# A state-space prologue on 64x64 quadrants of the PE array, with its input B laid out anew and ScalarE's early squares moved

## The chip, the cores and the metric

One core of a Trainium2 chip. The time is the device time of one execution in microseconds. Engines: PE (TensorE matmul), DVE (VectorE), ACT (ScalarE), POOL (GpSimd), SP (SyncE, which only issues DMAs; ACT issues some too).

## The reference, cut to what matters

T = 256 positions of 2048 channels pass through a state-space layer (S5), a SwiGLU feed-forward layer, a dilated attention layer and a second feed-forward layer. Only the first is touched:

```python
u = rms_norm(x, g)                       # 128 groups of 16 channels, 64 states a group
dt = exp(log_dt); a = exp(lam * dt)      # complex, worked out as pairs re, im
bb = ((a - 1) / lam)[..., None] * b      # den = lr*lr + li*li stands below the line
s[t] = a * s[t-1] + bb @ u[t]            # per group, an associative scan over t
y = Re(c @ s[t]) + d * u
z = gelu(y); val, gate = split(z @ w_glu)
x = x + val * sigmoid(gate)
```

## The kernel before, in words

The kernel is one program in a fixed order: each engine executes its instructions in the order in which the code writes them, and waits on semaphores in between. Its long part is `stream`, which reads each weight matrix in 128x1024 pieces, splits a piece into hi (ACT, L722 or L726) and lo (DVE), and does six matmuls of 512 columns per piece and half of T (`mm`, L744, L745, L748). The first job of the stream is GLU (`z @ w_glu`), and `later(d, f)` puts a task between its steps. The stream's loads begin during the prologue, at the calls `next(st)`.

Ahead of it is the prologue: `s5_load` (L191) issues the loads, `s5_params` (L238) works out a from lam and dt on DVE, and `s5` (L356) does the layer. The groups go in pairs, 64 pairs q in four sets k of 16; a tile has two halves of 64 partitions, g2, one per group of the pair. T is cut into 64 chunks of four positions, so that the scan runs over 64 chunk states `vs` (64 chunks, re and im, 64 pairs). The pieces:

- start: the parameters `par` (lam, log dt), B (`bt`, with the norm's gain `gb`), C (`ct`), x by rows (`xr`) and by channels (`xu`) are loaded; on ACT stand L371 (a negated copy of `gb`), four row squares L377 for the norm, L393, and then the two squares of lam, L259 (`den`) and L260 (`l2`), inside `s5_params`. On POOL stand memsets of zero blocks, the products L381 and L382 of B with the gain, and L387 (`dm`). DVE runs `exp_steps`: its third operation writes a bank that L259's tile shares.
- `w_build(k, q0, n)` (DVE, L447 to L457): per power j, two products and a sum, the matrices W.
- per unit u of 8 pairs: `v_trans` (PE transposes of W, ACT copies L466 and L467 into `wpad`, a half of the partitions each, zeros beside), `v_build` (PE L476, W times u; ACT copies L480 into `vs`).
- `q_build` (POOL, three operations per power t, `cmul`, L234 to L236): C times powers of a, into a `stage`, from which DMAs (L442) put each half into a tile `qp` with zero blocks.
- `k_build`, `t_build` (PE L493, then DMAs L510): the products inside a chunk, as a table `tz` per pair.
- the scan: `l1` (three levels inside four chunks), `l2` (one after another over 14 steps, small operations of 64 elements, L137), `l3` (three levels outward); `level` writes four operations, L523 to L526. `l1([3])` is POOL's. `coefs` (ACT, L551) copies the coefficients that DVE's scan reads into a bank.
- `t_part(k)` (PE L594) and `s_part(k)` (PE L608, gelu on ACT L610) sum y of a set into two banks; `z_part(k)` transposes z (PE L149), and splits it into hi (ACT L624) and lo (DVE).

Zero blocks make one matmul of 128 rows serve the two groups of a pair, which do not mix: with rows of both groups the columns of the other are zero. A `tile_position` of (0, 64h) puts it into one half of the array's columns.

The order at the end, on PE: t_part(0), t_part(1), s_part(0), z_part(0), s_part(1), t_part(2), t_part(3), s_part(2), s_part(3), GLU, with z_part(1) to z_part(3) as tasks inside GLU. On DVE: w_build, l1 of sets 0 and 1, l2(0) with l1 of 2, l3(0), l2(1) with l3(1), l3(2), l3(3). On POOL: q_build(0) and (1), l1([3]), q_build(2), q_build(3), one level of l3(3).

Of the kernel before, what the change touches and what calls it, by code (L numbers as in the profile page):

```python
# [55 lines left out]
def layouts(i):  # L56
# [5 lines left out]
    col = lambda v: np.broadcast_to(v.reshape(2, 1, 32, 2, 16), (2, 4, 32, 2, 16)).transpose(0, 1, 4, 2, 3).reshape(128, 64)  # L62
# [37 lines left out]
class Trunk:  # L100
# [90 lines left out]
    def s5_load(self):  # L191
# [8 lines left out]
        self.bt = za[:, 0:3072].rearrange("p (c r q) -> p c r q", c=16, r=3)  # L200
# [3 lines left out]
        nc.scalar.dma_start(self.bt[:, :, 0:2, :], a["bt"].rearrange("p (c r q) -> p c r q", c=16, r=2))  # L204
# [17 lines left out]
        pools = {True: [self.scr() for _ in range(2)], False: [self.wtile(w, F32) for w in ("hi", "lo", "lo")]}  # L222
# [14 lines left out]

    def s5_params(self, rms):  # L238
# [5 lines left out]
        homes = [[self.bank(i), 0] for i in (0, 1, 2, 3)]  # L244
        ins = self.small

        def ps(w):
            h = next(h for h in homes if h[1] + w <= 512)
            h[1] += w
            return h[0][:, h[1] - w:h[1]]  # L250

# [3 lines left out]
        zz, mags, k2, ang, l2, dens = [ins(64) for _ in range(6)]  # L255
        den, kk = ps(64), ps(64)
# [99 lines left out]
    def s5(self, st):  # L356
# [6 lines left out]
        wpad = self.p_x.tile([128, 2, 8, 2, 128], F32, tag="x", name="wpad")  # L363
        blank = lambda eng, v: [eng.memset(v[64 * g2:64 * g2 + 64, 2048 - 2048 * g2:4096 - 2048 * g2], 0.0) for g2 in range(2)]
# [28 lines left out]
        nc.scalar.activation(bt[:, :, 2, :], bt[:, :, 0, :], AF.Copy, scale=-1.0)  # L393
# [15 lines left out]
        for g2 in range(2):  # L409
            o = self.qp[64 * g2:64 * g2 + 64, 1, 2048 - 2048 * g2:4096 - 2048 * g2]  # L410
            nc.scalar.copy(o.rearrange("p (a b) -> p a b", b=64), bc(vs[64 * g2:64 * g2 + 64, 0, 0, :], [64, 32, 64], [1]))
# [16 lines left out]
        def q_build(k, ts):  # L428
# [4 lines left out]
            work = ptmp if k < 2 else [zb[:, 3072 + 512 * c:3584 + 512 * c] for c in range(2)]  # L433
            for t in ts:
                so = stage[k // 2][t // 2][:, 512 * (t % 2):512 * (t % 2) + 512]
                self.cmul(pool, v4(so), bc(self.lam[:, t, 1, qs], sh, [1, 1]),
                          bc(self.lam[:, t, 2, qs], sh, [1, 1]), ct[:, :, 1:3, qs], ct[:, :, 0:2, qs], v4(work[0]), v4(work[1]))
                if t % 2:
                    for g2 in range(2):
                        pr = slice(64 * g2, 64 * g2 + 64)  # L440
                        c = 2048 * g2 + 512 * t - 512
                        nc.sync.dma_start(qp[k][pr, c:c + 1024], stage[k // 2][t // 2][pr])  # L442

        stage = [[self.wtile(w, F32) for w in ("hi", "lo")]]
        w4 = lambda v, n: v[:, 0:32 * n].rearrange("p (c r q) -> p c r q", c=16, r=2)

        def w_build(k, q0, n):  # L447

            qs = slice(16 * k + q0, 16 * k + q0 + n)
            sh = [128, 16, 2, n]  # L450
            for j in range(5):
                if j < 4:
                    tt(w4(t1p[j % 2], n), bc(self.g[:, j, 0, qs], sh, [1, 1]), bt[:, :, 0:2, qs], mul)
                    tt(w4(dtmp[j % 2], n), bc(self.g[:, j, 1, qs], sh, [1, 1]), bt[:, :, 1:3, qs], mul)
                if j > 0:
                    tt(wt(k, q0, n)[:, :, :, j - 1, :].rearrange("p q r c -> p c r q"),
                       w4(t1p[(j - 1) % 2], n), w4(dtmp[(j - 1) % 2], n), add)  # L457

        def v_trans(u):
            k, e = u // 2, u % 2  # L460
            for f in range(2):
                ps = self.bank(f)
                for i in range(4):
                    self.tr(ps[:, 128 * i:128 * i + 128], wt(k, 8 * e + 4 * f + i)[:, 0].rearrange("p r j c -> p (r j c)"))
                pv4 = ps.rearrange("p (q m) -> p q m", q=4)
                nc.scalar.copy(wpad[0:64, e, 4 * f:4 * f + 4, 0, :], pv4[0:64])  # L466
                nc.scalar.copy(wpad[64:128, e, 4 * f:4 * f + 4, 1, :], pv4[64:128])  # L467

        def v_build(u):
# [12 lines left out]

        cd = usw.rearrange("p q n -> p (q n)")
        qp = [self.qp[:, 0], self.qp[:, 1], cd, self.qp[:, 0]]

        def k_build(k):

            h, b = k // 2, k % 2
            for i in range(16):
                o = kk[b][64 * h:64 * h + 64, 32 * i:32 * i + 32]  # L490
                for ri in range(2):
                    c0 = 64 * (16 * k + i) + 32 * ri
                    nc.tensor.matmul(o, wt(k, i)[:, 0, ri].rearrange("p j c -> p (j c)"), cd[:, c0:c0 + 32], start=False,  # L493
                                     stop=(i == 15 and ri == 1), tile_position=(0, 64 * h))
            nc.scalar.copy(kt[64 * h:64 * h + 64, :, b].rearrange("p g q c -> p q g c"),
                           kk[b][64 * h:64 * h + 64].rearrange("p (q g c) -> p q g c", q=16, g=2))

        def t_tile(t, n):

            for e in range(n // 16):  # L500
                nc.scalar.copy(t[:, 2048 * e:2048 * e + 2048].rearrange("p (a b) -> p a b", b=64),
                               bc(vs[:, 0, 0, :], [128, 32, 64], [1]))
            return t.rearrange("p (m q c) -> p m q c", m=8, c=16)

        def t_build(t, h, bs):
# [82 lines left out]
        def t_part(k, tz, nq):  # L588
            py = [self.bank(2 - 2 * (k % 2) + e) for e in range(2)]
# [557 lines left out]
```

## Time and profile before

| | before |
|---|---|
| median of 3 runs | 2258.2 us (2256.35 to 2258.35) |
| the profiled execution, its own time | 2256.78 us |
| its span in the trace | 2255.0 us |
| granted TensorE clock, mean | 0.99 of full speed |
| PE busy | 2154.6 us (96%) |
| DVE, ACT, POOL busy | 1546.1, 1035.3, 196.8 us |
| first matmul of GLU | at 170.15 us of the span |

Busy time is an average over the prologue and a stream more than ten times as long; POOL's 196.8 us lie almost all in the prologue. The trace counts two records for one fp32 matmul.

### The profile page before, as it was taken

How to read it: one execution, taken by the hardware profiler on the slowest of the kernel's cores; microseconds unless marked ns; L12 is line 12 of the kernel's file. 1: busy time of each engine (PE TensorE's matmuls, PEld its weight loads, DVE VectorE, ACT ScalarE, POOL GpSimd, SP SyncE). 2: the span in 40 equal slices, each digit the busy share in tenths (PEclk: the TensorE clock that was granted, in tenths of full speed). 3: DMA queues.
4: the chain of work that ended last, by engine and by line, in shares of the span. 5: the costliest groups of instructions: out<-in, count | busy, mean ns of one | idle time of the engine just before them, and what ended most of it. 6: DMA issues, size and time to landing. Idle time of an engine off the chain costs nothing.

```text
span 2255.0 us, 27355 instructions
## 1 busy us (share of the span) xinstructions
PE 2154.6 (96%) x10520; PEld 1791.5 (79%) x10520; DVE 1546.1 (69%) x2648; ACT 1035.3 (46%) x1177; POOL 196.8 (9%) x166
## 2 busy tenths in 40 slices
PE   1769999999999999999999999999999999999998
PEld 1658888888888888878888888877888888888886
DVE  7785777776777675574877687677776776774544
ACT  3714445444444443433545545535444444444443
POOL 6930000000000000000000000000000000000000
PEclk9979999999999999999999999999999999999999
DMA  5425555555555555555554444445555555555553
GB/s 166 109 88 206 190 189 214 187 188 204 187 188 201 191 202 190 186 187 195 191 186 177 143 173 159 150 167 181 193 189 203 189 191 199 188 214 196 201 188 131
DMA packets 60563, 410.37 MB, mean 182 GB/s; under 512 B 7248, under 2 KB 8144, under 8 KB 12816
## 3 DMA queue, kind: packets, MB, share of 16 engines
q1 hardware_dynamic: 58176, 400.13, 49.8%
q10 hardware_dynamic: 1968, 6.92, 0.9%
q8 instruction: 82, 1.34, 0.2%
q0 software_dynamic: 288, 1.57, 0.2%
q14 instruction: 49, 0.40, 0.1%
HBM read 398.90 MB, written 2.10 MB: 178 GB/s over the span
## 4 chain that ended last, share of the span: by engine, by line
PE 88%; DVE 8%; issue 2%; ACT 1%; DMA 1%; SPq 0%; ACTq 0%; DVEq 0%
PE b L745 28%; PE b L744 28%; PE b L748 28%; DVE scr L814 2%; DVE lo L137 1%; PE b L608 1%; DVE b L137 1%; PE b L149 1%; PE b L1037 1%; ACT hi L722 1%; DMA qp<-in_xr 1%; DVE raw L137 1%; PE b L1068 1%; DVE b L523 0%; DVE b L525 0%
## 5 line engine op out<-in xcount | busy, mean ns | idle before, releaser
L146 DVE SCALAR_TENSOR_TENSOR lo<-raw,gcol,hi 128x1024 fp32r<-128x1024 f32 x464 | 594.5, 1291 | 324.2 <-ACT hi L726 318.1
L744 PE MATMUL b<-hi,xt 128*128 128x512 f32 x1856 | 726.2, 391 | 1.7 <-ACT hi L726 1.4
L745 PE MATMUL b<-lo,xt 128*128 128x512 f32 x1856 | 722.7, 389 | 0.9 <-DVE lo L146 0.9
L726 ACT ACTIVATE hi<-raw,gcol 128x1024 fp32r<-128x1024 f32 x464 | 525.1, 1148 | 398.3 <-PE b L748 378.1
L748 PE MATMUL b<-hi,xt 128*128 128x512 f32 x1856 | 571.8, 389 | 0.0
L137 DVE TENSOR_TENSOR lo<-raw,hi 128x1024 fp32r<-128x1024 f32 x272 | 335.7, 1239 | 304.4 <-ACT hi L722 303.0
L722 ACT CAST hi<-raw 128x1024 fp32r<-128x1024 f32 x272 | 283.5, 1052 | 315.3 <-PE b L748 305.9
L744 PEld LDWEIGHTS b<-hi,xt 128*128 128x128 f32 x1856 | 348.5, 188 | 73.8 <-ACT hi L726 1.8
L748 PEld LDWEIGHTS b<-hi,xt 128*128 128x128 f32 x1856 | 348.4, 188 | 73.1
L745 PEld LDWEIGHTS b<-lo,xt 128*128 128x128 f32 x1856 | 348.5, 188 | 72.5 <-DVE lo L146 1.8
L745 PE MATMUL b<-lo,ht 128*128 128x512 f32 x704 | 274.3, 390 | 2.5 <-DVE lo L137 2.5
L744 PE MATMUL b<-hi,ht 128*128 128x512 f32 x704 | 274.0, 389 | 0.1
L814 DVE STREAM_TRANSPOSE scr<-scr 32x128 f32<-32x128 f32 x704 | 212.9, 302 | 11.3
L748 PE MATMUL b<-hi,ht 128*128 128x512 f32 x704 | 217.2, 389 | 0.0
L745 PEld LDWEIGHTS b<-lo,ht 128*128 128x128 f32 x704 | 132.1, 188 | 31.5 <-DVE lo L137 4.0
L744 PEld LDWEIGHTS b<-hi,ht 128*128 128x128 f32 x704 | 132.1, 188 | 27.7 <-ACT hi L722 0.5
L748 PEld LDWEIGHTS b<-hi,ht 128*128 128x128 f32 x704 | 132.1, 188 | 27.5
L818 POOL TENSOR_TENSOR ht<-scr,ht 128x512 fp32r<-128x512 f32 x44 | 57.0, 1296 | 880.9 <-ACT ht L817 852.4
L817 ACT CAST ht<-scr 128x512 fp32r<-128x512 f32 x44 | 27.3, 621 | 178.5 <-DVE scr L814 178.5
L745 PE MATMUL b<-lo,z 128*128 128x512 f32 x256 | 100.1, 391 | 0.5 <-DVE lo L137 0.5
L814 DVE STREAM_TRANSPOSE scr<-x 32x128 f32<-32x128 f32 x320 | 96.8, 302 | 4.9
L744 PE MATMUL b<-hi,z 128*128 128x512 f32 x256 | 100.0, 391 | 0.0
(205 smaller groups left out, 1475.2 us busy)
## 6 DMA issues: line engine op xcount, KB each, us to landing
raw<-in_fi SPq DMA_DIRECT2D x176, 1024.0 KB, 4.8
raw<-in_fo SPq DMA_DIRECT2D x88, 1024.0 KB, 4.8
raw<-in_wq SPq DMA_DIRECT2D x48, 1024.0 KB, 4.8
raw<-in_glu SPq DMA_DIRECT2D x32, 1024.0 KB, 4.8
raw<-in_wo SPq DMA_DIRECT2D x16, 1024.0 KB, 4.8
raw<-in_kv SPq DMA_DIRECT2D x8, 1024.0 KB, 4.8
qp<-in_xr SPq DMA_DIRECT2D x4, 512.0 KB, 10.9
xw<-in_xu SPq DMA_DIRECT2D x4, 512.0 KB, 11.3
```

Of the source, the lines that this page charges most:

```text
L137: self.nc.vector.tensor_tensor(out, in0, in1, op)
L146: self.nc.vector.scalar_tensor_tensor(out, in0, s, in1, op0, op1)
L149: self.nc.tensor.transpose(out, in_, self.ident[:n, :n])
L608: nc.tensor.matmul(py[e][64 * h:64 * h + 64, 128 * i:128 * i + 128], vs[:, :, ri, 16 * k + q], w[:, :, ri, q], start=False, stop=(i == 3 a ...
L722: nc.scalar.copy(hi, raw)
L726: nc.scalar.activation(hi, raw, AF.Copy, scale=gk)
L744: nc.tensor.matmul(ps[b], xh, hi[:, c], start=first, stop=False)
L745: nc.tensor.matmul(ps[b], xh, lo[:, c], start=False, stop=False)
L748: nc.tensor.matmul(ps[b], xl, hi[:, c], start=False, stop=last)
L814: nc.vector.transpose(out[32 * q:32 * q + 32, :, 32 * a:32 * a + 32], src[32 * a:32 * a + 32, :, q, :])
L817: nc.scalar.copy(dst(0), out)
L818: nc.gpsimd.tensor_tensor(dst(1), out, dst(0).bitcast(F32), ALU.subtract)
```

## The change

**Quadrants.** `v_build`, `k_build`, `t_part` and `s_part` use 64 rows and 64 columns of the array for each matmul (`tile_position=(64*row, 64*col)`), one group of a pair in each row half, so there are no zero blocks: `wpad` becomes `wT` (two copies of 128x512 per unit in place of four of 64x512), and `cd` (an input of 2 MB), its four DMAs, the fills of `tz`, `qp` and `cd` by ACT are gone. The columns that a matmul streams halve (128 to 64 in `t_part` and `s_part`; 32 to 16 in `k_build`), and there are twice as many. A bank now belongs to a row half g2, and gelu reads by g2.

**Q in place.** `q_build` writes straight into `qp` (four sets in two tiles of half size) with no stage and no DMA.

**B laid out for W.** `bt` goes from (c, r, q) to (r, q, c): the DMA is 8 KB a row, and `w_build`'s operations run over 16 adjacent elements in c.

**ACT.** `s5_homes` holds the squares of lam ahead of L371's copy and the row squares; `coefs(0)` comes after unit 3.

**Order.** q_build(0), (1), (2), then l1([3]), then q_build(3) on POOL; t_part(2) behind s_part(0), t_part(3) behind s_part(1); z_part(0) and z_part(1) ahead of s_part(2), through bank 5 alone, with a full copy on ACT and lo on POOL; z_part(2) and (3) as tasks of GLU; `next(st)` earlier; two of l3(3)'s levels as 8 operations of 480 elements for 16 of 240.

The diff's core (`k_build`, `t_build` and `v_trans` follow the same pattern):

```diff
 def s5_load
-        nc.scalar.dma_start(self.bt[:, :, 0:2, :], a["bt"].rearrange("p (c r q) -> p c r q", c=16, r=2))
+        nc.scalar.dma_start(za[:, 0:2048], a["bt"])
...
+    def s5_homes(self):
...
+        self.den, self.li2 = ps(64), self.small(64)
+        self.nc.scalar.activation(self.den, self.par[:, 0:64], AF.Square)
+        self.nc.scalar.activation(self.li2, self.par[:, 64:128], AF.Square)
...
 def s5_params
-        nc.scalar.activation(den, lr, AF.Square)
-        nc.scalar.activation(l2, li, AF.Square)
...
 def s5
-        pool.memset(wpad[0:64, :, :, 1, :], 0.0)
-        pool.memset(wpad[64:128, :, :, 0, :], 0.0)
-        blank(pool, self.qp[:, 0])
+        pool.memset(tz, 0.0)
         nc.scalar.activation(self.rq[:, 0:1], vs[:, 0, 0, 0:1], AF.Sqrt)
+        self.s5_homes()
+        nc.scalar.activation(ngb, self.gb, AF.Copy, scale=-1.0)
...
         def w_build(k, q0, n):
-                    tt(w4(t1p[j % 2], n), bc(self.g[:, j, 0, qs], sh, [1, 1]), bt[:, :, 0:2, qs], mul)
+                    tt(w4(t1p[j % 2], n), bc(self.g[:, j, 0, qs], sh, [2, 2]), bq[:, qs, 0:2], mul)
-                    tt(wt(k, q0, n)[:, :, :, j - 1, :].rearrange("p q r c -> p c r q"),
-                       w4(t1p[(j - 1) % 2], n), w4(dtmp[(j - 1) % 2], n), add)
+                    tt(wt(k, q0, n)[:, :, :, j - 1, :], w4(t1p[(j - 1) % 2], n), w4(dtmp[(j - 1) % 2], n), add)
...
         def v_build(u):
+                    for g2 in range(2):
+                        nc.tensor.matmul(pv[ri][half(g2), 64 * i:64 * i + 64], wT[e][half(ri), i, half(g2)],
+                                         (upp if ri == g2 else usw)[half(ri), q0 + i, :], start=True, stop=True,
+                                         tile_position=(64 * ri, 64 * g2))
...
+            if u == 3:
+                coefs(0, 5)
+        coefs(1, 7)
+        for k in range(3):
+            q_build(k)
         go(l1([0, 1], dve))
...
         go(l1([3], pool))
+        q_build(3)
...
         def t_part
-                        nc.tensor.matmul(py[e][64 * h:64 * h + 64, 128 * i:128 * i + 128], upp[:, q, :], tz[:, :, q % nq, :],
-                                         start=(i == 0), stop=False, tile_position=(0, 64 * h))
+                        for g2 in range(2):
+                            nc.tensor.matmul(py[g2][half(h), 64 * (4 * e + i):64 * (4 * e + i) + 64], upp[half(g2), q, :],
+                                             th[k // 2][half(g2), :, 16 * (q % 32):16 * (q % 32) + 16],
+                                             start=(e == 0 and i == 0), stop=False, tile_position=(64 * g2, 64 * h))
...
         def s_part
-                            nc.tensor.matmul(py[e][64 * h:64 * h + 64, 128 * i:128 * i + 128], vs[:, :, ri, 16 * k + q],
-                                             w[:, :, ri, q], start=False, stop=(i == 3 and ri == 1), tile_position=(0, 64 * h))
+                            for g2 in range(2):
+                                nc.tensor.matmul(py[g2][half(h), 64 * (4 * e + i):64 * (4 * e + i) + 64],
+                                                 vs[half(g2), :, ri, 16 * k + q], qv[k][half(g2), :, ri, q], start=False,
+                                                 stop=(e == 1 and i == 3 and ri == 1), tile_position=(64 * g2, 64 * h))
...
         def z_part
+                if copy:
+                    nc.scalar.copy(full, src)
+                    pool.tensor_tensor(low, full, hi.bitcast(F32), sub)
...
         s_part(0, py[0])
-        q_build(3, range(4))
-        lo = z_part(0, (7, 2))
-        l31 = l3(1)
-        go(l2(1), l31)
-        go(lo)
+        py.append(t_part(2, 2))
+        go(l2(1), l3(1))
         s_part(1, py[1])
-        py += [t_part(2, tq[0], 16), t_part(3, tq[1], 16)]
-        next(st)
+        py.append(t_part(3, 0))
         go(l3_level(3, 3, pool))
         go(l3(2))
-        go(pipe([l3_level(3, i, dve, q0, 8) for q0 in (0, 8) for i in range(1, 3)]))
+        for k in range(2):
+            z_part(k, (5, 5), True)
         s_part(2, py[2])
+        go(pipe([l3_level(3, i, dve) for i in range(1, 3)]))
         next(st)
         s_part(3, py[3])
```

The first rows of ACT. Names: `hi_84` holds the parameters, `lo_88` is gb, `z_86` bt, `qp` the rows of x. Before:

```order
L370 ACT_TABLE_LOAD
L370 ACTIVATE rq<-vs 128x1
L371 ACTIVATE z_86<-lo_88 128x1024
L377 ACTIVATE qp,ss<-qp 128x1024 x4
L393 ACTIVATE z_86<-z_86 128x16x64
L259 ACTIVATE b_129<-hi_84 128x64
L260 ACTIVATE hi_108<-hi_84 128x64
```

With the change:

```order
L368 ACT_TABLE_LOAD
L368 ACTIVATE rq<-vs 128x1
L245 ACTIVATE b_114<-hi_84 128x64
L246 ACTIVATE hi_108<-hi_84 128x64
L370 ACTIVATE z_86<-lo_88 128x1024
L376 ACTIVATE qp,ss<-qp 128x1024 x4
L391 ACTIVATE z_86<-z_86 128x1024
```

The two squares of lam (L259, L260; now L245, L246) have moved from behind six operations to the front.

POOL where l1([3]) begins (`vs` is the chunk states, `lo_249` and `lo_243` the working tile, `scr` holds coefficients and powers). Before:

```order
L234 TENSOR_TENSOR lo_249<-scr_106,z_87 128x512
L235 TENSOR_TENSOR lo_249<-scr_106,z_87 128x512
L236 TENSOR_TENSOR lo_253<-lo_249 128x512
L523 TENSOR_TENSOR lo_249<-scr_107,vs 128x512
L524 TENSOR_TENSOR lo_249<-scr_107,vs 128x512
L525 TENSOR_TENSOR lo_249<-lo_249,vs 128x512
L526 TENSOR_TENSOR vs<-lo_249 128x16x2x16
```

With the change:

```order
L230 TENSOR_TENSOR lo_243<-scr_106,z_87 128x512
L231 TENSOR_TENSOR lo_243<-scr_106,z_87 128x512
L232 TENSOR_TENSOR qp<-lo_243 128x512
L508 TENSOR_TENSOR lo_243<-scr_107,vs 128x512
L509 TENSOR_TENSOR lo_243<-scr_107,vs 128x512
L510 TENSOR_TENSOR lo_243<-lo_243,vs 128x512
L511 TENSOR_TENSOR vs<-lo_243 128x16x2x16
```

What is written is now `qp` and not the stage, and 36 such operations of `q_build` stand ahead of l1([3]) where there were 24.

ACT at the end of the prologue (`xw` receives z, `z_1157` and `z_1509` hi of z; L610 and L598 are gelu). Before:

```order
L610 ACTIVATE xw<-b_972 128x8x4x16
L610 ACTIVATE xw<-b_973 128x8x4x16
L624 CAST z_1157<-b_1158 128x512
L624 CAST z_1157<-b_1164 128x512
L610 ACTIVATE xw<-b_990 128x8x4x16
L610 ACTIVATE xw<-b_991 128x8x4x16
L610 ACTIVATE xw<-b_1274 128x8x4x16
L610 ACTIVATE xw<-b_1275 128x8x4x16
L722 CAST hi_1382<-raw_1310 128x1024
```

With the change:

```order
L598 ACTIVATE xw<-b_1111 128x8x4x16
L598 ACTIVATE xw<-b_1112 128x8x4x16
L614 CAST z_1509<-b_1510 128x512
L617 COPY xw<-b_1510 128x512
L614 CAST z_1509<-b_1518 128x512
L617 COPY xw<-b_1518 128x512
L614 CAST z_1509<-b_1526 128x512
L617 COPY xw<-b_1526 128x512
L614 CAST z_1509<-b_1534 128x512
L617 COPY xw<-b_1534 128x512
L598 ACTIVATE xw<-b_1291 128x8x4x16
```

The gelu of set 1 (b_1111, b_1112) is now followed by four pairs of copies, two for each of z_part(0) and z_part(1), ahead of the gelu of set 2 (b_1291); before, two copies of z_part(0) stood ahead of the gelu of set 1 (b_990).

## Rows read from the trace of the kernel before

**Rows 1.** The page, 40 equal slices of the span, two engines.

```profile
PE   1769999999999999999999999999999999999998
...
POOL 6930000000000000000000000000000000000000
```

**Rows 2.** PE in order of time, 140 to 171 us (start, length, line, count, releaser).

```profile
140.82 1.94 PE L149 MATMUL b<-cst,xw 128*128 128x128 f32 x8 [7.92 <-DVE b L137]
144.22 7.71 PE L608 MATMUL b<-qp,vs 128*64 128x128 f32 x64 [1.46 <-DVE vs L526]
151.67 3.76 PE L594 MATMUL b<-raw,xw 128*64 128x128 f32 x64
...
170.15 0.50 PE L744 MATMUL b<-hi,z 128*128 128x512 f32 x1
```

**Rows 3.** Order of time on DVE, 30 to 160 us.

```profile
35.28 0.43 DVE L137 TENSOR_TENSOR b<-b,z 128x256 f32<-128x256 f32 x1
...
71.46 1.12 DVE L137 TENSOR_TENSOR z<-b,dtmp 128x256 f32<-128x256 f32 x2
83.45 0.70 DVE L523 TENSOR_TENSOR b<-b,vs 128x512 f32<-128x512 f32 x1 [10.86 <-ACT b L551]
...
125.08 0.67 DVE L523 TENSOR_TENSOR b<-b,vs 128x480 f32<-128x480 f32 x1
```

**Rows 4.** Order of time on DVE, 0 to 20 us.

```profile
4.44 1.98 DVE L143 TENSOR_SCALAR hi<-hi 128x64 f32<-128x64 f32 x2 [4.44 <-DMA hi<-in_par]
17.11 0.23 DVE L141 TENSOR_SCALAR b<-hi 128x64 f32<-128x64 f32 x1 [10.69 <-ACT b L259]
17.37 1.47 DVE L141 TENSOR_SCALAR hi<-hi 128x64 int32<-128x64 int32 x1
...
18.89 0.18 DVE L141 TENSOR_SCALAR hi<-hi 128x64 int32<-128x64 int32 x1
```

**Rows 5.** Order of time on ACT and its issues (ACTq), 0 to 182 us.

```profile
1.94 4.87 ACTq L205 DMA_DIRECT2D cst<-in_consts  x1
6.85 1.28 ACT L370 ACT_TABLE_LOAD   x1 [6.85 <-issue]
...
16.87 0.21 ACT L259 ACTIVATE b<-hi 128x64 f32<-128x64 f32 x1
...
82.08 0.34 ACTq L648 DMA_DIRECT2D xw<-in_cd  x1
...
141.95 0.59 ACT L624 CAST z<-b 128x512 fp32r<-128x512 f32 x1 [8.41 <-PE b L149]
```

**Rows 6.** Order of time on POOL, 0 to 52 us.

```profile
11.85 2.35 POOL L381 TENSOR_TENSOR z<-z,lo 128x1024 f32<-128x1024 f32 x1 [3.64 <-DMA z<-in_bt]
...
16.86 1.92 POOL L387 TENSOR_TENSOR lo<-cst,hi 128x1024 f32<-128x1024 f32 x1
```

**Rows 7.** Groups by shape, 0 to 175 us (count, busy us, mean ns, idle before).

```profile
L466 ACT COPY wpad<-b 64x512 f32<-64x512 f32 x16 | 9.5, 595 | 5.3 <-PE b L149 5.1
...
L137 DVE TENSOR_TENSOR raw<-b,dtmp 128x512 f32<-128x512 f32 x8 | 8.1, 1046 | 0.0
...
L526 DVE TENSOR_TENSOR vs<-b,dtmp 128x512 f32<-128x512 f32 x6 | 4.1, 678 | 0.0
```

**Rows 8.** Order of time on POOL, 50 to 99 us.

```profile
50.29 1.27 POOL L234 TENSOR_TENSOR lo<-scr,z 128x512 f32<-128x512 f32 x1
...
83.17 1.27 POOL L523 TENSOR_TENSOR lo<-scr,vs 128x512 f32<-128x512 f32 x1 [1.44 <-ACT vs L480]
...
97.08 1.20 POOL L526 TENSOR_TENSOR vs<-lo 128x480 f32<-128x480 f32 x1
```

**Rows 9.** PE at 71 us; L608 by stretch (busy, count, granted clock, DMA share, GB/s).

```profile
71.51 2.09 PE L476 MATMUL b<-xw,wpad 128*64 128x64 f32 x64 [0.40 <-ACT vs L480]
...
125.10:127.00 1.90, 1.90 (x16) 0.50 0.00 0
157.00:160.00 3.00, 3.00 (x29) 1.00 1.02 391
```

More of the change, by code (lines that the diff above doesn't have):

```diff
@@ L221, in s5_load @@
         nc.sync.dma_start(self.gcol, a["gcol"])
-        pools = {True: [self.scr() for _ in range(2)], False: [self.wtile(w, F32) for w in ("hi", "lo", "lo")]}
+        pools = {True: [self.scr() for _ in range(2)], False: [self.wtile(w, F32) for w in ("hi", "lo")]}
         used = {k: [0] * len(v) for k, v in pools.items()}
@@ L236, in cmul, with ps @@
         eng.tensor_tensor(out, t1, t2, ALU.add)
+    def s5_homes(self):
+        homes = [[self.bank(i), 0] for i in (0, 1, 2, 3)]
+        def ps(w):
+            h = next(h for h in homes if h[1] + w <= 512)
+            h[1] += w
+            return h[0][:, h[1] - w:h[1]]
+        self.psmall = ps
+        self.den, self.li2 = ps(64), self.small(64)
+        self.nc.scalar.activation(self.den, self.par[:, 0:64], AF.Square)
+        self.nc.scalar.activation(self.li2, self.par[:, 64:128], AF.Square)
     def s5_params(self, rms):
@@ L243, in s5_params @@
         I = lambda v: v.bitcast(I32)
[L244 to L250, printed above, removed]
+        ins, ps, den, l2 = self.small, self.psmall, self.den, self.li2
         lr, li, ldt = self.par[:, 0:64], self.par[:, 64:128], self.par[:, 128:192]
@@ L392, in s5 @@
         r = self.r
[L393 removed]
+        nc.scalar.activation(bt[:, 2], bt[:, 0], AF.Copy, scale=-1.0)
         def rms():
@@ L426, in s5, with q_build @@
         cp = self.cp
-        def q_build(k, ts):
+        bq = bt.rearrange("p r (q c) -> p q r c", c=16)
+        qv = [self.qp[:, k // 2, 2048 * (k % 2):2048 * (k % 2) + 2048].rearrange("p (m r q) -> p m r q", r=2, q=16)
+              for k in range(4)]
+        def q_build(k):
             qs = slice(16 * k, 16 * k + 16)
@@ L464, in v_trans @@
                     self.tr(ps[:, 128 * i:128 * i + 128], wt(k, 8 * e + 4 * f + i)[:, 0].rearrange("p r j c -> p (r j c)"))
-                pv4 = ps.rearrange("p (q m) -> p q m", q=4)
-                nc.scalar.copy(wpad[0:64, e, 4 * f:4 * f + 4, 0, :], pv4[0:64])
-                nc.scalar.copy(wpad[64:128, e, 4 * f:4 * f + 4, 1, :], pv4[64:128])
+                nc.scalar.copy(wT[e][:, 4 * f:4 * f + 4, :], ps.rearrange("p (q m) -> p q m", q=4))
+        half = lambda n: slice(64 * n, 64 * n + 64)
@@ L483, in s5 @@
[L483 to L490, printed above, removed]
-                for ri in range(2):
[L492 to L505, printed above, removed]
+            pv = [self.bank(2 + ri) for ri in range(2)]
+            for i in range(8):
+                for ri in range(2):
+                    for g2 in range(2):
+                        nc.tensor.matmul(pv[ri][half(g2), 64 * i:64 * i + 64], wT[e][half(ri), i, half(g2)],
+                                         (upp if ri == g2 else usw)[half(ri), q0 + i, :], start=True, stop=True,
+                                         tile_position=(64 * ri, 64 * g2))
@@ new lines, in v_build, with k_build @@
+            for ri in range(2):
+                nc.scalar.copy(vs[:, 1:64, ri, q0:q0 + 8].rearrange("p n q -> p q n"),
+                               pv[ri].rearrange("p (q n) -> p q n", q=8)[:, :, 0:63])
+        def k_build():
+            kk = [self.bank(g2) for g2 in range(2)]
+            for g2 in range(2):
+                nc.tensor.matmul(kk[g2], self.ident, dm[:, 512 * g2:512 * g2 + 512], start=True, stop=False)
+            for i in range(32):
+                for ri in range(2):
+                    for h in range(2):
+                        q = 32 * h + i
+                        for g2 in range(2):
+                            nc.tensor.matmul(kk[g2][half(h), 16 * i:16 * i + 16],
+                                             wt(q // 16, q % 16)[half(g2), 0, ri].rearrange("p j c -> p (j c)"),
+                                             ct[half(g2), :, 1 + ri, q], start=False, stop=(i == 31 and ri == 1),
+                                             tile_position=(64 * g2, 64 * h))
+            for g2 in range(2):
+                nc.scalar.copy(kt[:, g2], kk[g2])
@@ L507, in t_build @@
+        def t_build(h):
             for jp in range(4):
@@ L586, in s5, with t_part @@
         zs = {}
-        def t_part(k, tz, nq):
-            py = [self.bank(2 - 2 * (k % 2) + e) for e in range(2)]
+        def t_part(k, b):
+            py = [self.bank(b + g2) for g2 in range(2)]
             for e in range(2):
@@ L612, in s_part, with z_part @@
             zs[k] = z.rearrange("p j i g c -> p j (i g c)")
-        def z_part(k, bs=(7, 6)):
+        def z_part(k, bs, copy):
             zf, lo = zs[k], []
@@ L621, in z_part @@
                     self.tr(pt[:, 128 * j:128 * j + 128], zf[:, j, 128 * e:128 * e + 128])
-                dst = lambda hl, e=e: self.zv(k, hl).rearrange("p k (j n) -> p k j n", j=4)[:, 2 * e:2 * e + 2]
+                v = lambda x, e=e: x.rearrange("p k (j n) -> p k j n", j=4)[:, 2 * e:2 * e + 2]
+                hi, low = [v(self.zv(k, hl)) for hl in range(2)]
                 src = pt.rearrange("p (j h n) -> p h j n", j=4, h=2)
-                nc.scalar.copy(dst(0), src)
-                lo.append(lambda dst=dst, src=src: tt(dst(1), src, dst(0).bitcast(F32), sub))
+                nc.scalar.copy(hi, src)
+                if copy:
+                    full = v(usw[:, 16 * k:16 * k + 16, :].rearrange("p q n -> p (q n)").rearrange("p (k t) -> p k t", k=4))
+                    nc.scalar.copy(full, src)
+                    pool.tensor_tensor(low, full, hi.bitcast(F32), sub)
+                else:
+                    lo.append(lambda low=low, src=src, hi=hi: tt(low, src, hi.bitcast(F32), sub))
             return lo
@@ L645, in s5 @@
             v_build(u)
-            if u % 2:
-                c = slice(512 * u - 512, 512 * u + 512)
-                nc.scalar.dma_start(cd[:, c], a["cd"][:, c])
-                q_build(u // 4, ((u - 1) % 4, u % 4))
-        coefs(0, 7)
-        coefs(1, 5)
-        go(l1([0, 1], dve))
-        kk = [self.bank(b) for b in range(2)]
-        for b in range(2):
-            nc.tensor.matmul(kk[b], self.ident, dm[:, 512 * b:512 * b + 512], start=True, stop=False)
-        tz = t_tile(self.p_x.tile([128, 4096], F32, tag="x", name="tz"), 32)
@@ L657, in s5 @@
-        kt = za[:, 0:1024].rearrange("p (g b q c) -> p g b q c", g=2, b=2, q=16)
-        go(l1([3], pool))
-        k_build(0)
-        k_build(1)
-        t_build(tz, 0, slice(0, 2))
-        k_build(2)
-        k_build(3)
-        tq = [t_tile(self.rawtile(), 16) for _ in range(2)]
-        for b in range(2):
-            t_build(tq[b], 1, slice(b, b + 1))
-        py = [t_part(0, tz, 32), t_part(1, tz, 32)]
-        stage.append([v for r in [self.rawtile()] for v in (r[:, 0:1024], r[:, 1024:2048])])
@@ L669, in s5 @@
-        for g2 in range(2):
-            nc.scalar.copy(cd[64 * g2:64 * g2 + 64, 2048 - 2048 * g2:4096 - 2048 * g2],
-                           bc(vs[64 * g2:64 * g2 + 64, 0, 0, :], [64, 64, 32], [2]))
+            if u == 3:
[3 more added lines that the diff above has]
+            q_build(k)
+        go(l1([0, 1], dve))
+        kt = za[:, 0:1024].rearrange("p (g x) -> p g x", g=2)
+        th = [tz[:, 2048 * h:2048 * h + 2048].rearrange("p (m x) -> p m x", m=4) for h in range(2)]
@@ L672, in s5 @@
+        k_build()
+        go(l1([3], pool))
+        q_build(3)
+        t_build(0)
+        t_build(1)
+        next(st)
+        py = [t_part(0, 2), t_part(1, 0)]
         go(l2(0), l1([2], dve))
-        q_build(2, range(4))
         go(l3(0))
         s_part(0, py[0])
-        q_build(3, range(4))
-        lo = z_part(0, (7, 2))
-        l31 = l3(1)
-        go(l2(1), l31)
-        go(lo)
+        py.append(t_part(2, 2))
+        go(l2(1), l3(1))
         s_part(1, py[1])
-        py += [t_part(2, tq[0], 16), t_part(3, tq[1], 16)]
@@ L683, in s5 @@
-        next(st)
-        ptmp = [zb[:, 3072 + 512 * c:3584 + 512 * c] for c in range(2)]
+        py.append(t_part(3, 0))
         go(l3_level(3, 3, pool))
         go(l3(2))
-        go(pipe([l3_level(3, i, dve, q0, 8) for q0 in (0, 8) for i in range(1, 3)]))
+        for k in range(2):
+            z_part(k, (5, 5), True)
         s_part(2, py[2])
+        go(pipe([l3_level(3, i, dve) for i in range(1, 3)]))
         next(st)
         s_part(3, py[3])
-        for k in range(1, 4):
-            lo = []
-            self.later(2 * k - 2, lambda k=k, lo=lo: lo.extend(z_part(k)))
-            self.later(2 * k - 1, lambda lo=lo: go(lo))
+        lo = []
@@ L695, in s5 @@
+        self.later(0, lambda: z_part(2, (7, 6), True))
+        self.later(2, lambda: lo.extend(z_part(3, (7, 6), False)))
+        self.later(3, lambda: go(lo))
         self.x = self.p_x.tile([128, 2, 2048], F32, tag="x", name="x")
```

80 lines of the change are left out of this document (28 added, 52 removed).

## Prediction

> **What bounds the kernel now.** I read the page's slices first, then each engine's order of time in the first 182 us, then the groups of instructions by shape. The slices [rows 1] show two regimes. From the fourth slice on PE is busy nine tenths or more: that is the weight stream, which the change hardly touches. In the first three (56 us each) POOL works, as nowhere later, and PE waits. The stream begins with the first L744 at 170.15 us [rows 2], so the time is 170.15 plus some 2085 us, and the question is how far the change moves that 170.15.
>
> I follow the prologue back from there. PE runs s_part(1), t_part(2), t_part(3), s_part(2), s_part(3) in one row from 144.22 to 170.15 [rows 2], 25.9 us. s_part(1) waited for DVE, which at 125.08 began the scan levels l2(1) and l3(1) [rows 3]. Before them DVE worked from 83.45 without a gap: l1 of pairs 0 and 1, l2(0) with l1 of pair 2, l3(0), together 41.6 us. At 83.45 it had been idle for 10.86 us, for ACT's copy L551 (coefs): w_build had ended at 72.6, having begun at 35.28 [rows 3]. I call that beginning T0; the stream starts at T0+134.9. T0 comes late: after two operations DVE waited 10.69 us for the square L259 on ACT [rows 4], and ACT, held by the issue of the DMA L205 from 1.94 to 6.81, did the scaling L371 and four row squares L377 first and reached L259 at 16.87 [rows 5].
>
> **Step 1, T0.** The two squares of lam go ahead of L371 and the row squares. They need only the parameters, landed by 4.44 [rows 4]. The issue of L205 was long because, as I read it, it stood behind the transfer of B in 512-byte pieces; as 8 KB rows an issue costs some 0.4 us, as the one of cd at 82.08 did with 0.34 [rows 5]. With ACT free at about 2.4 and 1.28 for the table load, L259 is done at about 4.9 instead of 17.1: 12.2 us earlier. DVE's next integer shift took 1.47 us, against 0.18 for its like at 18.89 [rows 4], while POOL was in L387 (16.86 to 18.78) [rows 6]. That is one stall of 1.3 us gone with its cause. But the chain now runs from 5 to some 20 us, beside L381 and its like L382, 2.35 each, and L387, 1.92 [rows 6], on POOL, which start when B has landed. Each can hold back such a DVE operation, at most for its own length: 6.6 in all, and I take 4.0, as a stalled operation starts inside its POOL neighbour. So T0 = 35.3 − 12.2 − 1.3 + 4.0 = 25.8, taken as 26.0, **−9.3 us**. Bounds: 24.2 with 2.3 of stall; 31.4 if ACT is held as before (L259 then at 8.5, 8.4 us gained) and all 6.6 of the stalls fall in.
> The Trainium skill ("Advanced Engine Details and Errata", VectorE Performance Modes) says that VectorE's second port is shared with GpSimd and that two-port operations and GpSimd's block each other. The trace agrees with its 1.47 against 0.18; without it one would write 0 in place of 4.0, and the sum would be 4 us lower.
>
> **Step 2, T0 to l2(1).** DVE's own work: w_build writes its sums in runs of 16 elements. Its eight 128x512 sums took 1046 ns where the scan's sums of that size, written in such runs, took 678 [rows 7]. I take 678: −2.9 us for those eight, and for the sixteen half as large (0.56 each, 71.46 [rows 3]) the same share, 35%, −3.2; 37.3 becomes 31.2. (Lower end: the products, which now read in runs of 16, stay as they are; upper end 37.3.) The wait of 10.86 goes: coefs(0) is copied after the fourth unit, by when ACT is through it sooner too, since each of its eight units does two copies of whole height where it did four of 0.595 [rows 7]. Then 41.6 us as before. DVE would reach l2(1) at T0+72.8.
> **But l2(1) also needs l1 of pair 3, which POOL does**, and q_build(2) now stands ahead of it. POOL began q_build at 50.29, T0+15.0, did 24 operations up to 81.73 (83.17 less the idle 1.44; 1.31 each), then l1([3]) from 83.17 to 98.28, 15.1 [rows 8]. With 36 in front that is 15.0 + 47.2 + 15.1 = T0+77.3. So what is late next is POOL, 4.5 us after DVE, and a slow w_build (up to T0+78.9) would hide behind it but for 1.6. Before, l2(1) stood at T0+89.8: **−12.4 us**.
> What I cost at nothing here: the DMAs for Q and for cd, removed from SP and ACT; k_build and t_build, which begin when w_build's last unit is through ACT, some T0+38, and have until s_part(0) at T0+73; s_part(0) and t_part(2), which have from there to s_part(1) at T0+96; the earlier loads of the stream's first weights, whose casts ACT does only behind s_part(2). The cover is DVE's and POOL's scan: a slip of these counts only past s_part(1), some 20 us later.
>
> **Step 3, l2(1) to s_part(1).** The same DVE operations, 19.1 us: 0. s_part(1) starts at T0+96.5.
>
> **Step 4, the tail on PE.** It is now s_part(1), its two gelus, t_part(3) (into the same banks), z_part(0) and z_part(1) through a single bank, s_part(2), s_part(3). s_part(1) was 64 records in 7.71 us, 120 ns each, and hardly other at the granted clock 0.50 (1.2 GHz; 16 in 1.90 us) than at 1.00 (2.4 GHz; 29 in 3.00) [rows 9], where the contiguous t_part of the same 128 columns took 3.76 [rows 2]: so it is bound by the strided reading, and that stays. The quadrants have twice the records with half the columns. If both row halves read at once, that is 64 columns at 60 ns for each of 64 pairs, 3.9 us; bounds 3.4 (pairs at t_part's spacing) and 7.7 (halves in turn). I take 3.9, because the pairs of v_build L476 ran 64 records in 2.09 [rows 9], 33 ns each, hence tiles do run side by side. Two gelus of 0.60 with their start: 1.5. t_part(3): half of 3.76, 1.9. The z_parts are four round trips: four transposes (8 took 1.94 [rows 2], so up to 1.0; t_part's 59 ns a record gives 0.5) and two copies of 0.59 [rows 5], 2.3 in all; three whole ones and the last's transposes, 7.6. Then two s_parts, 7.8. Sum: 3.9 + 1.5 + 1.9 + 7.6 + 7.8 = 22.7 against 25.9: **−3.2 us**. DVE's l3(2) and l3(3) end at T0+104 and T0+109, ahead of s_part(2) at T0+111.4 and s_part(3) at T0+115.
>
> **Step 5, in the stream.** z_part(1) no longer stands between the stream's matmuls; its 8 transposes of 128 columns are worth up to 1.94, at t_part's 59 ns a record 0.5; in between: **−0.9 us**. The rest is the same stream.
>
> Sum: −9.3 − 12.4 − 3.2 − 0.9 = −25.8. The profiled execution took 2256.8 (span 2255.0), so 2231.0 beside it; the median of the runs shown is 2258.2, 1.4 above it, and I predict **2232**.
>
> **The rivals.**
> *A, the row halves take turns.* s_part's reading is the bound, and nothing in the trace shows two row halves at once: all tiles there are column halves over 128 rows. Then each s_part stays 7.7, three of them on the path cost +11.4: 2244. Against it: the two halves read different partitions.
> *B, the quadrants do not overlap at all.* A weight load for a quadrant waits for the matmul that is running, and 128 records of an s_part go one after another at 115 ns, the spacing of strided records [rows 9]: 14.7 us each, 3 × 10.8 = +32.4, 2264, **slower by 6**. It decides from 12.5 us each (3.9 + 25.8/3). Against it: the 33 ns of L476, two tiles of one row group. The Trainium skill ("TensorE: Matmul & The Clock Gate", Part 3: Packing small matmuls) says that a load overlaps matmuls in flight only when its row group differs. By that rule L476 could not have overlapped; the trace differs, and so I give B little.
> *C, the parameter chain gains less.* ACT stays held by its DMA issue and POOL's products stall DVE fully: T0 = 31.4, +5.4, and the other terms stand: 2238. For it: why L205 took 4.87 us to issue is inferred.
>
> **How the numbers follow.** Chances: forecast 0.67, A 0.12, C 0.12, B 0.06, and 0.03 for A and C together with a slow w_build, which would come near no change. A measurement of this kernel can tell about 0.2%, 4.5 us, from no change. Forecast, A and C lie below that: faster 0.91; same 0.03; slower is B, 0.06. The forecast's own range is 2226 to 2238: down by 1.8 (T0 24.2), 1.5 (three s_parts at 3.4) and some 3 if the transposes are warm and the round trips 1.8; up by T0's bound. To take in A it reaches to 2245; B stays outside.
>
> **What would show it.** DVE's third operation at 5 us, not 17; w_build from about 26; no wait of 10 us ahead of l1; the last POOL operation of l1([3]) releasing DVE's l2(1); s_part groups of 128 records in 3.9 us; four round trips of PE and ACT; L744's successor at 145 us. Wrong it would be if s_part's records stay 120 ns apart in 128 of them (A or B), if the square on ACT still comes after 8 us (C), or if something else than POOL releases l2(1).

## The result, and the profile after

| | before | changed |
|---|---|---|
| median | 2257.99 us (4 runs) | 2226.61 us (4 runs, 2226.03 to 2229.92) |
| profiled execution, its own time | 2256.78 us | 2226.55 us |
| its span | 2255.0 us | 2224.7 us |
| GLU's first matmul | 170.15 us | 140.77 us |

The ratio is 0.9865, 95% interval 0.9848 to 0.9883: 31.4 us faster. The forecast was 2232, in a range from 2225 to 2245. The span is 30.3 us shorter: the stream behind GLU's first matmul takes 2083.9 us, 0.9 less than before, and the other 29.4 lie in the prologue.

ACT in order of time, changed kernel (start, length, line, operation, idle before and releaser), to be set beside [rows 5]:

```profile
1.65 0.45 ACTq L201 DMA_DIRECT2D cst<-in_consts  x1
2.14 1.28 ACT L368 ACT_TABLE_LOAD   x1 [2.14 <-issue]
...
4.10 0.23 ACT L245 ACTIVATE b<-hi 128x64 f32<-128x64 f32 x1 [0.46 <-DMA hi<-in_par]
```

The issue of the constants takes 0.45 us, not 4.87, and the square that stood at 16.87 stands at 4.10. DVE in order of time, beside [rows 3, 4]:

```profile
4.77 0.23 DVE L137 TENSOR_SCALAR b<-hi 128x64 f32<-128x64 f32 x1
...
10.94 1.27 DVE L139 TENSOR_SCALAR hi<-hi 128x64 int32<-128x64 int32 x1
...
13.32 1.20 DVE L139 TENSOR_SCALAR hi<-hi 128x64 f32<-128x64 f32 x1
...
23.71 0.43 DVE L133 TENSOR_TENSOR b<-b,z 128x256 f32<-128x256 f32 x1
...
55.47 0.69 DVE L508 TENSOR_TENSOR b<-b,vs 128x512 f32<-128x512 f32 x1
...
97.09 0.67 DVE L508 TENSOR_TENSOR b<-b,vs 128x480 f32<-128x480 f32 x1
100.87 0.23 DVE L133 TENSOR_TENSOR b<-b,vs 128x64 f32<-128x64 f32 x1 [3.12 <-POOL vs L511]
```

The third operation comes at 4.77 with no wait. T0, the beginning of w_build, is 23.71 for 35.28. Two operations of the chain take 1.27 and 1.20 where their like took 0.2. l1 begins at 55.47 without the wait of 10.86; at 97.09 DVE does its one free operation of l3(1) and then waits 3.12 us for POOL. POOL in order of time, beside [rows 6, 8]:

```profile
9.82 2.34 POOL L379 TENSOR_TENSOR z<-z,lo 128x1024 f32<-128x1024 f32 x1 [5.44 <-DMA z<-in_bt]
12.13 2.34 POOL L380 TENSOR_TENSOR z<-z 128x1024 f32<-128x1024 f32 x1
...
38.70 1.26 POOL L230 TENSOR_TENSOR lo<-scr,z 128x512 f32<-128x512 f32 x1
...
85.76 1.26 POOL L508 TENSOR_TENSOR lo<-scr,vs 128x512 f32<-128x512 f32 x1
...
99.62 1.22 POOL L511 TENSOR_TENSOR vs<-lo 128x480 f32<-128x480 f32 x1
```

Here are the neighbours of the two slow DVE operations (L379 and L380), then the 36 operations of q_build from 38.70 and l1([3]) from 85.76; its last operation ends at 100.84, and DVE goes on at 100.87. The groups by shape on DVE:

```profile
L133 DVE TENSOR_TENSOR raw<-b,dtmp 128x512 f32<-128x512 f32 x8 | 5.3, 679 | 0.0
...
L133 DVE TENSOR_TENSOR raw<-b,dtmp 128x256 f32<-128x256 f32 x8 | 3.1, 413 | 0.0
```

w_build's sums fell from 1046 ns [rows 7] to 679, those of half the size from 560 [rows 3] to 413. PE in order of time at the end, beside [rows 2]:

```profile
119.54 4.24 PE L592 MATMUL b<-qp,vs 64*64 64x64 f32 x128 [15.70 <-DVE b L133]
124.47 0.32 PE L580 MATMUL b<-tz,xw 64*64 64x64 f32 x2 [0.69 <-ACT xw L598]
124.96 1.16 PE L580 MATMUL b<-tz,xw 64*64 64x64 f32 x62 [0.16 <-ACT xw L598]
126.05 0.66 PE L145 MATMUL b<-cst,xw 128*128 128x128 f32 x4
127.87 0.66 PE L145 MATMUL b<-cst,xw 128*128 128x128 f32 x4 [1.16 <-ACT xw L617]
129.69 0.66 PE L145 MATMUL b<-cst,xw 128*128 128x128 f32 x4 [1.16 <-ACT xw L617]
131.51 1.12 PE L145 MATMUL b<-cst,xw 128*128 128x128 f32 x4 [1.16 <-ACT xw L617]
132.55 8.29 PE L592 MATMUL b<-qp,vs 64*64 64x64 f32 x256
140.77 0.50 PE L724 MATMUL b<-hi,z 128*128 128x512 f32 x1
```

s_part(1) is 4.24 us for 128 records; t_part(3), the four round trips of z_part(0) and z_part(1), which start 1.82 us apart, s_part(2) and s_part(3) follow, and GLU.

### The profile page after: what moved, and what is told of

Read it like the earlier page. It is cut to its first block, busy times and chain, and to the rows that moved or that the text cites. A ratio compares the mean times of both kernels' runs of the same rounds, so it can differ in the third digit from the quotient of the medians.

```text
span 2224.7 us, 28537 instructions
## 1 busy us (share of the span) xinstructions
PE 2133.0 (96%) x11160; PEld 1769.2 (80%) x11160; DVE 1536.1 (69%) x2634; ACT 1011.8 (45%) x1157; POOL 200.6 (9%) x169
## 4 chain that ended last, share of the span: by engine, by line
PE 88%; DVE 6%; POOL 3%; issue 2%; ACT 1%; DMA 0%; ACTq 0%; DVEq 0%; POOLq 0%
PE b L725 28%; PE b L728 28%; PE b L724 28%; DVE scr L794 2%; DVE lo L133 1%; PE b L145 1%; POOL qp L232 1%; POOL lo L230 1%; POOL lo L231 1%; PE b L1017 1%; ACT hi L702 1%; PE b L592 1%; PE b L1048 1%; POOL xw L411 0%; PE b L1019 0%
## 5 line engine op out<-in xcount | busy, mean ns | idle before, releaser
L725 PEld LDWEIGHTS b<-lo,ht 128*128 128x128 f32 x704 | 132.2, 188 | 31.2 <-DVE lo L133 4.1
```

Source lines behind the costliest of these rows:

```text
L725: nc.tensor.matmul(ps[b], xh, lo[:, c], start=False, stop=False)
```

## The experiments

Each edits the changed kernel, but for `r10_before_squares`, which edits the kernel before. T0 is again the beginning of w_build. Where nothing else is said, a time is a median, compared with the changed kernel's 2226.6, whose four runs spread over 3.9 us.

**The squares put back** (`r1_squares_late`).

```diff
-        self.s5_homes()
         nc.scalar.activation(ngb, self.gb, AF.Copy, scale=-1.0)
...
+        self.s5_homes()
         self.s5_params(rms)
```

> The changed kernel with one thing put back: ACT does the two squares of lam behind the scaled copy and the four row squares, as before; B keeps its new layout. My theory (the order of ACT's first operations carries step 1): DVE's third operation waits until about 16 us in place of 4.8, less one or two stalls beside GpSimd, so w_build begins some 10 us later (33.5 for 23.7) and everything behind it shifts with it: slower than the changed kernel by 9 to 10.5 us, about 2236. Rival (the short DMA issue carries it, the order little): slower by 0 to 3 us.

2236.8 us, 10.2 above the changed kernel. DVE in order of time:

```profile
16.10 0.23 DVE L137 TENSOR_SCALAR b<-hi 128x64 f32<-128x64 f32 x1 [11.45 <-ACT b L245]
...
33.79 0.43 DVE L133 TENSOR_TENSOR b<-b,z 128x256 f32<-128x256 f32 x1
```

T0 is 33.79, 10.1 later, and the time follows it. The order on ACT carries this, even where no issue is long.

**B in pieces** (`r2_b_pieces`).

```diff
-        nc.scalar.dma_start(za[:, 0:2048], a["bt"])
+        nc.scalar.dma_start(za[:, 0:2048].rearrange("p (x d) -> p x d", x=16),
+                            a["bt"].rearrange("p (x d) -> p x d", x=16)[:, :, 0:128])
```

> The changed kernel, with B padded in memory so that its load goes in 2048 pieces of 512 bytes again; the layout on chip and the order on ACT stay. My theory (the pieces held ACT's next DMA issue): the issue of the constants takes about 5 us again, the table load begins near 7, the squares near 8.5, w_build near 27.5: slower by 3 to 4.5 us than the changed kernel. Rival (the long issue had another cause, such as the number of issues): the issue stays under 1 us and the time within 1 us.

2238.4 us, 11.8 above. ACT and its issues, then DVE:

```profile
1.18 0.68 ACTq L200 DMA_DIRECT2D z<-in_bt  x1
1.89 10.73 ACTq L201 DMA_DIRECT2D cst<-in_consts  x1
...
14.06 0.21 ACT L245 ACTIVATE b<-hi 128x64 f32<-128x64 f32 x1
```

```profile
18.24 2.24 DVE L137 TENSOR_SCALAR hi<-hi 128x64 int32<-128x64 int32 x1
...
20.79 2.27 DVE L137 TENSOR_SCALAR hi<-hi 128x64 int32<-128x64 int32 x2
...
35.58 0.43 DVE L133 TENSOR_TENSOR b<-b,z 128x256 f32<-128x256 f32 x1
```

The next issue takes 10.73 us, more than twice what I expected and than the kernel before had; B lands late too (L379 at 18.09 for 9.82), and each of L379 and L380 holds back a DVE operation for nearly its whole length. T0 is 35.58. So the pieces, not the count of issues, hold ACT; the size was missed. Here the pieces lie apart in memory and side by side on the chip, in the kernel before it was the other way round, which may be why it is more; that was not taken further.

**The squares alone, in the kernel before** (`r10_before_squares`): `s5_homes` as in the change, called ahead of L371.

> The kernel before with one part of the change alone: ACT's two squares of lam ahead of the scaled copy and the row squares. B keeps its old layout, so the issue of the constants holds ACT until 6.8 and the squares come near 8.4. My theory: w_build begins earlier by 8.5 less what GpSimd's products now hold back on DVE (2 to 5 us): 4 to 7 us earlier, and all behind it shifts alike, 2250.5 to 2253.5. Rival (the wait of 10.86 us for the coefficients swallows it, because ACT is late for reasons of its own): within 1.5 us of the kernel before.

2253.8 us, ratio to the kernel before 0.9983 (0.9974 to 0.9992). DVE:

```profile
8.35 0.23 DVE L141 TENSOR_SCALAR b<-hi 128x64 f32<-128x64 f32 x1 [1.91 <-ACT b L249]
...
11.58 2.45 DVE L143 TENSOR_SCALAR hi<-hi 128x64 f32<-128x64 f32 x2
...
14.41 1.94 DVE L141 TENSOR_SCALAR hi<-hi 128x64 int32<-128x64 int32 x1
...
16.66 2.02 DVE L141 TENSOR_SCALAR hi<-hi 128x64 int32<-128x64 int32 x2
...
30.84 0.43 DVE L137 TENSOR_TENSOR b<-b,z 128x256 f32<-128x256 f32 x1
```

The wait for the square falls from 10.69 to 1.91, but three groups beside POOL's products take 2.45, 1.94 and 2.02, and T0 gains 4.4 of the 8.8 us. The two parts of the change need each other: the reordering alone gives 4 us, and in `r1_squares_late`, with the layout but not the order, T0 comes only 1.5 us earlier than in the kernel before; together they give 11.6.

**coefs(0) put back** (`r3_coefs_late`): `coefs(0, 5)` behind the loop over units.

> The changed kernel with coefs(0) put back behind the eight units. My theory (GpSimd's l1 of set 3 is what releases l2(1), and DVE has 3.1 us of slack there): l1 on DVE starts near 65 in place of 55.5, DVE reaches l2(1) near 107.4 where GpSimd is done at 100.9: slower by about 6.5 us, the delay of 9.7 less the slack. Rivals: DVE alone is the bound, slower by 9.7; or GpSimd has more slack than seen, slower by 0 to 2.

2232.7 us, 6.1 above. DVE:

```profile
64.44 0.70 DVE L508 TENSOR_TENSOR b<-b,vs 128x512 f32<-128x512 f32 x1 [8.89 <-ACT b L536]
```

l1 begins 9.0 us later, and less the slack of 3.1 that is 5.9. The wait that POOL ends is gone in this run.

**l1([3]) first on POOL** (`r4_l1_first`).

```diff
-        for k in range(3):
+        for k in range(2):
             q_build(k)
...
         go(l1([3], pool))
+        q_build(2)
         q_build(3)
```

> The changed kernel with l1 of set 3 ahead of q_build(2) on GpSimd. My theory: the wait of 3.12 us that DVE has for it disappears, DVE is the bound, and Q of set 2 is still done some 30 us before it is read: faster by 3.1 us, about 2223.5. Rival (something else than GpSimd released l2(1), or the row of the wait is an artefact): no difference within 0.5 us.

The wait is gone and s_part(1) starts at 116.36 for 119.54, as expected; the profiled run's span is 3.1 us shorter. PE:

```profile
116.36 4.25 PE L592 MATMUL b<-qp,vs 64*64 64x64 f32 x128 [12.48 <-DVE b L133]
```

The median is 2224.96, 1.65 below, in runs from 2223.2 to 2228.0; the intervals overlap. The mechanism is shown, its worth by this run alone is not.

**Q's columns adjacent** (`r5_q_contig`).

```diff
-.rearrange("p (m r q) -> p m r q", r=2, q=16)
+.rearrange("p (r q m) -> p m r q", r=2, q=16)
```

> The changed kernel with Q laid out as (re/im, pair, column), so that the 64 columns that a matmul of s_part streams are adjacent; the weights, vs, stay at a stride of 512 bytes, and GpSimd's sums now write with a stride of 128 bytes in place of runs. Theory M (the streamed side is the bound of s_part): s_part falls from 4.24 to some 2.0 to 2.3 us for 128 records, three of them on the path, so 6 to 6.6 us less at the end, if GpSimd's sums keep their 1.27 us. Theory W (the strided weight load is the bound): s_part stays at 4.2 and the time within 1 us of the changed kernel. If GpSimd's strided writes are slower, its l1 of set 3 comes later by twelve times the difference, which adds to either.

2225.6 us, 1.05 below, within the spread of the runs; POOL's sums keep their 1.28 us. PE:

```profile
119.66 3.81 PE L592 MATMUL b<-qp,vs 64*64 64x64 f32 x128 [15.40 <-DVE b L133]
...
132.42 7.41 PE L592 MATMUL b<-qp,vs 64*64 64x64 f32 x256
```

s_part falls from 4.24 to 3.81, far less than the 2.0 to 2.3 of theory M. So the streamed side is not the only bound: with its stride gone, something else holds s_part at 3.8. That this is the stride of the weights, as theory W has it, is what is left over and not shown: weights laid adjacent were not tried, as the scan writes them.

**Row halves in turn** (`r6_rows_outer`): the loop over g2 outermost in s_part.

> The changed kernel with s_part's loop over the row half outermost: the 64 records of one half first, then the 64 of the other, the same matmuls. My theory (the two row halves read at once only if their matmuls alternate): 7.5 to 7.7 us per s_part in place of 4.24, three on the path, slower by about 10 us, 2237. Rival (the bound is a count of records or of weight loads, not which half reads): s_part stays at 4.2 to 4.5 and the time within 1 us.

2240.5 us, 13.9 above. PE, then DVE:

```profile
121.74 7.45 PE L592 MATMUL b<-qp,vs 64*64 64x64 f32 x122 [11.75 <-DVE b L133]
...
129.12 0.43 PE L592 MATMUL b<-qp,vs 64*64 64x64 f32 x4
130.25 1.98 PE L580 MATMUL b<-tz,xw 64*64 64x64 f32 x62 [0.70 <-ACT xw L598]
132.15 1.11 PE L145 MATMUL b<-cst,xw 128*128 128x128 f32 x4
...
139.12 15.05 PE L592 MATMUL b<-qp,vs 64*64 64x64 f32 x256
```

```profile
9.66 2.45 DVE L137 TENSOR_SCALAR hi<-hi 128x64 int32<-128x64 int32 x2
...
13.53 0.88 DVE L139 TENSOR_SCALAR hi<-hi 128x64 int32<-128x64 int32 x1
...
15.53 1.17 DVE L139 TENSOR_SCALAR hi<-hi 128x64 f32<-128x64 f32 x1
```

s_part(1) takes 7.45 us for 122 of its 128 records and 7.8 for all, the other two 7.5 each, as rival A had it: the halves overlap only if their matmuls alternate. With the row half the bank changes too (`py[g2]`), and no run separates the two. The three s_parts give 10.3 us. Another 2.2 lie at the start: T0 is 25.89, because the parameters landed 0.5 us later and three DVE operations, not two, fell beside POOL's: the integer shifts beside L379 (2.45 us for the two), then one of 0.88 beside L380 and one of 1.17 beside L385. The rest, about 1.6 in the profiled run, lies where the granted clock was 0.50 (the 1.2 GHz level) and not 1.00 as in the changed kernel: 62 records of t_part(3) took 1.98 us for 1.16, the first transposes 1.11 for 0.66, and GLU's first matmuls 0.63 for 0.40.

**z_part(0) earlier** (`r7_z0_early`).

```diff
         s_part(0, py[0])
+        z_part(0, (2, 3), True)
         py.append(t_part(2, 2))
...
-        for k in range(2):
-            z_part(k, (5, 5), True)
+        z_part(1, (5, 5), True)
```

> The changed kernel with z_part(0) between s_part(0) and t_part(2), on banks 2 and 3, where PE waits some 15 us for DVE; z_part(1) stays ahead of s_part(2) on bank 5. My theory (each round trip of transposes and two copies through one bank, 1.82 us by the trace, is on the path): faster by two of them, 3.6 us, about 2223; s_part(2) then starts near 128.9, 2 us after DVE's l3(2) ends. Rival (s_part(2) waits for DVE anyway): faster by under 1 us.

PE:

```profile
102.79 1.09 PE L145 MATMUL b<-cst,xw 128*128 128x128 f32 x8 [1.18 <-ACT xw L598]
...
126.19 0.66 PE L145 MATMUL b<-cst,xw 128*128 128x128 f32 x4
128.01 0.66 PE L145 MATMUL b<-cst,xw 128*128 128x128 f32 x4 [1.16 <-ACT xw L617]
128.59 8.29 PE L592 MATMUL b<-qp,vs 64*64 64x64 f32 x256
```

s_part(2) starts at 128.6 for 132.5 and the span is 4.1 shorter in the profiled run; the median, 2224.67, is 1.9 below, and the intervals overlap: again the mechanism is shown, its worth by this run alone is not.

**Joined** (`r8_joined`: r4 and r7, with z_part(1) a task of GLU, and z_part(2) and z_part(3) as later tasks, all three without the full copy; `r9_joined_q`: with r5 as well).

> The changed kernel with l1 of set 3 ahead of q_build(2), z_part(0) between s_part(0) and t_part(2), and z_part(1) as a task of GLU. My theory: s_part(1) starts 3.1 us earlier, near 116.4; s_part(2) then waits for DVE's l3(2), near 123.6, and s_part(3) for l3(3), near 128.8; GLU starts near 133 in place of 140.8, and 0.8 us of z_part(1) come back in the stream: faster than the changed kernel by about 7 us, 2219.5. Rival (the two gains share a wait, or z_part(1) in the stream stalls its first steps): faster by 3 to 5 us.

> The same with Q's columns adjacent, as in r5. My theory: the 0.4 us that it takes off an s_part count for s_part(1) and for s_part(3), the other is hidden by DVE: 0.5 to 1 us below r8_joined. Rival (s_part(2) and s_part(3) both wait for DVE): within 0.5 us of it.

2220.5 us (ratio to the kernel before 0.9836, 0.9823 to 0.9850) and 2219.3 us (0.9831, 0.9818 to 0.9845), 6.1 and 7.3 below the changed kernel; r9's interval lies wholly below the changed kernel's, r8's but for its end. The 1.2 us between the two lie within their intervals. PE in r8_joined:

```profile
124.40 4.31 PE L592 MATMUL b<-qp,vs 64*64 64x64 f32 x128 [1.38 <-DVE vs L511]
129.18 4.33 PE L592 MATMUL b<-qp,vs 64*64 64x64 f32 x128 [0.47 <-DVE vs L511]
133.44 0.50 PE L724 MATMUL b<-hi,z 128*128 128x512 f32 x1
```

GLU starts at 133.44, 7.3 earlier, and s_part(2) and s_part(3) now wait 1.38 and 0.47 us for DVE's scan: DVE binds to the end of the prologue. The stream behind takes 2085.3 us for 2083.9, so 1.3 come back where 0.8 were expected.

## Why the prediction was right, point by point

The time lies in the range, near its lower end, 5.4 us under the forecast; of the spans, −30.3 where −25.8 was worked out. The path and its waits came as told, and three of the four terms came out larger than forecast.

- **Step 1** (−9.3): measured −11.6. The mechanism is as told (r1, r2, r10). The term mis-sized is the stall of 4.0: the two slow operations cost 2.1 in all, since L385 met none. How much is lost depends on which operation stands there: in r6, where L385 met one too, the three slow groups cost about 3.8 (2.45, 0.88 and 1.17, less some 0.7 alone). So the 2.1 is in part luck. The Trainium skill ("Advanced Engine Details and Errata", VectorE Performance Modes) says that GpSimd's instructions and two-port ones of VectorE block each other; the trace agrees here too, with the 1.27 and 1.20 beside L379 and L380.
- **Steps 2 and 3** (−12.4): measured −13.1, from T0 to s_part(1). POOL's end at T0+77.3 came at T0+77.1; w_build took 31.8 for 31.2, as its sums of half the size fell by 26% and not by 35%; DVE's slack was 3.1 for 4.5. r3 and r4 confirm that POOL releases l2(1).
- **Step 4** (−3.2): measured −4.7 (21.2 us). The three s_parts took 12.5 for 11.7, but the four round trips 6.5 for 7.6, since the transposes of three took the short time, 0.66, and the gelus with t_part(3) 2.3 for 3.4, since t_part(3) starts beside the second gelu. Part of this is luck of the clock: t_part(3) and those transposes ran at the granted clock 1.00 here, t_part(3) and the first transposes at 0.50 in r6 (1.98 and 1.11 us).
- **Step 5** (−0.9): measured −0.9. In r8, with z_part(1) among GLU's tasks again, the stream takes 1.3 more.
- **Rivals.** A and B fall with the 4.24; r6 shows A's price when the halves do take turns. In r6, with one half after the other, the records of s_part follow at 59 ns each (15.05 us for 256), half of B's 115, while a weight load's record lasts 207 ns there. Under the Trainium skill's rule ("TensorE: Matmul & The Clock Gate", Part 3) loads of one row group would not overlap its matmuls. By these records the trace differs from the rule. C's cause is real (r2) and was absent. C's T0 of 31.4 does not follow from its own terms: 35.3 − 8.4 − 1.3 + 6.6 is 32.2, which would put C at 2238.2 and changes nothing else.
- **A reason that was half right:** I called s_part bound by the strided reading of 64 columns, and meant the streamed side. It fits that a record took 120 ns with 128 streamed columns and 59 with 64 (r6), at 64 columns of weights in both. But r5 shows a second bound just behind it: with the streamed columns adjacent, s_part is still 3.81. That this is the weights' stride is argued, not shown.

## What to carry to other kernels

Read what a wait will turn into: after the coefficients' wait went, the next bound, POOL's queue, was readable from counts of operations to 0.2 us. Where blocks of 64 do not mix, four quadrants in place of zero blocks nearly halve a matmul group (7.71 to 4.24), if consecutive matmuls alternate between row halves and, as here, their banks (7.5 to 7.8 if not). A small operation at the head of a long chain goes first in its queue, but a long DMA issue in front of it can take the gain back (r2: T0 at 35.58).

## What the runs showed that was not expected

- A DMA of 512-byte pieces held the next issue of the same engine for 10.73 us, against 0.45 behind 8 KB rows.
- Runs of one kernel differ by up to 4.8 us (2226.0 to 2229.9; r4 2223.2 to 2228.0). r6's profile shows one source, a stall of DVE beside POOL that depends on a landing 0.5 us earlier or later. The profiles of r3 and r6 show another: with t_part(3) and the first transposes at the granted clock 0.50, the stretch from s_part(1)'s end to s_part(2) takes 10.1 and 9.6 us for 8.8. How much of the spread either makes was not measured.
